# Attention scores: the low-key matmuls of two heads in the two halves of the TensorE array

## The chip, the cores and the metric

The kernel runs on one core of a Trainium2 chip. TensorE (PE) multiplies, VectorE (DVE), ScalarE (ACT) and GpSimd (POOL) do the elementwise work, SyncE (SP) and the others issue the DMAs. The metric is the device time of one launch in microseconds (us); before the change its median over 3 runs was 724.25 us (724.15 to 724.58).

## What is computed

One decoder block over 512 positions of 1024 channels, in float32. The part that the change touches is the attention with three kinds of keys (8 heads of 64 channels, two groups of 4 heads that share keys):

```python
def masked_softmax(s, mask):
    p = jax.nn.softmax(jnp.where(mask, s, NEG), axis=-1)
    return jnp.where(mask, p, 0.0)

# for a block of 128 query positions:
sc = einsum('bqghd,bkgd->bghqk', qc, k_cmp) * scale       # compressed keys
p_c = masked_softmax(sc, cmp_end <= t);  o_c = einsum(p_c, v_cmp)
...
ss = einsum('bqghd,bgqkd->bghqk', qc, ks) * scale         # selected blocks of keys
p_s = masked_softmax(ss, kpos <= t);     o_s = einsum(p_s, vs)
...
sw = einsum('bqghd,bkgd->bghqk', qc, kw) * scale          # sliding window of keys
p_w = masked_softmax(sw, mask_w);        o_w = einsum(p_w, vw)
out = gc[..., 0:1] * o_c + gc[..., 1:2] * o_s + gc[..., 2:3] * o_w
```

With 512 positions there are 8 blocks of 64 keys and up to 16 may be selected, and the window is 512 wide, so both branches see all keys up to the query; they differ in their keys and values. Around this stand a gated short convolution, a merge of the two mixers, and a feed-forward layer with a convolution (2816 channels).

## The kernel before

Precision comes from splitting: a float32 value becomes a high part (a rounded copy) and a low part (the rest), and a product is the sum of high x high, low x high and high x low. The helper `dense` does so with three matmuls per unit (lines 140, 143, and 145 or 147).

For scores, the 64 channels of a head fill only half of the array's 128 rows, and the query operand uses both halves: tile `q` (in the trace `qT`) holds for each head the high part of the query in one half of the partitions, `own`, and the low part in the other. Group 0 has its high part in the lower half, group 1 in the upper half. The keys lie in `kk`: `kHH` has the high part of the keys in both halves, and `kL` has the low part in the half where the query's high part lies and zeros in the other, written by two memsets (line 584). So two matmuls give a head's scores (`scores`, lines 714 and 715): q against `kHH` makes high x high + low x high in one pass, and q against `kL` makes high x low.

The operands are made in `qkv`, token tile by token tile (128 positions, `tt` 0 to 3): transposes into PSUM (`pqt`, line 681), then for each group a copy of the high part (ACT, 686), a subtraction for the low part of the query (DVE, 689), two copies of the keys' high part (ACT, 692 and 693), and a subtraction for the keys' low part (DVE, 694). The compressed keys are made once in `compress` (lines 623 to 625).

`attend(pt_, g, qt)` handles one group and one query tile; tiles go in the order 3, 2, 1, 0. Tile 3 has 512 keys, tile 2 384, and in tiles 2 and 1 the branch 0 takes the 32 compressed keys with it (416 and 288 columns); tile 3 makes its compressed scores apart (`pcm`, line 725), and tile 0 does both branches in one matmul (line 753). Each head's scores take one of three PSUM banks `s` (`s_bank`). `exps` adds the causal mask (DVE, 741), takes the maximum (DVE, 742) and the exponential (ACT, 743), which frees the bank. Then the weights are scaled (769), transposed (`pt`, 792), split (`ph` 795, `pl` 796) and multiplied by the values (800 to 805). The compressed weights take a way of their own (`xs` 782, `ptc` 785).

The framework's scheduler sets the order of instructions on each engine ahead of time, from program order and simulated times; `behind(later, earlier)` adds an order without a semaphore, and `tc.high_priority()` raises an instruction's place. During attention PE also does the convolution's products (`pa`), the merge gates (`pg`) and the mixer's output (`pma`), which need nothing of attention. Of the last gate before the merge (`gate_tile(KD + 4)`) three units are ordered behind the last transposes and value products of attention (`HOLD_PTC`, `HOLD_PT`, `HOLD_PO`).

Of the kernel before, what the change touches and what calls it, by code (L numbers as in the profile page):

```python
# [11 lines left out]
F32 = mybir.dt.float32  # L12
F32R = mybir.dt.float32r
I32 = mybir.dt.int32
AF = mybir.ActivationFunctionType
# [9 lines left out]
G = 2  # L25
HG = H // G
HD = 64
# [7 lines left out]
NC = S // STRIDE  # L35
# [56 lines left out]
def tile_block(ctx: ExitStack, tc: tile.TileContext, xT, pos, par, par2, w_tok, w_a3, w_gate, w_ao, w_bo, w_o,  # L92
               w_ff, w_dn, c_w1, out):
    nc = tc.nc
# [28 lines left out]
    def s_bank(name):  # L123
        return bank("s", name, 3)
# [8 lines left out]
    loads, splits = [], []  # L133
# [186 lines left out]
    def behind(later, earlier):  # L320

        tc.add_manual_dep(later.ins, earlier.ins.name,
                          mybir.DependencyInfo(mybir.DependencyClass.NoSync, mybir.DependencyReason.DATA),
                          reason="order")
# [204 lines left out]
    kHH, kL = kk[:, 0], kk[:, 1]  # L529
    kl4 = kL.rearrange("p (b g) s -> p b g s", g=G)  # L530
# [22 lines left out]
    def compress():  # L553

        ph = s_bank("ph")
        hb = w_tmp("hb", (7, 2 * NC))
        z, e, hid = (hb[:, i] for i in range(3))
        peb = pp.tile([P, 1], F32, name="peb", tag="peb")

        half = 2 * G * (NC + 1)  # L560
        hl = ph[:, 0:2 * half].rearrange("p (s n) -> p s n", s=2)
        blocks = kc2s.rearrange("p b s a k g -> p b s (a k g)")
        for i in range(2):
            wh, wl = load_w(c_w1[:, :, 8 * i:8 * i + 8], D, f"w1{i}", mixed=True)
            for n in range(8):
                x = blocks[:, n, :, 2 * G * i:2 * G * i + half]
                c = slice(n * P, (n + 1) * P)
                nc.tensor.matmul(hl, wh[:, c], x, start=i + n == 0, stop=False)
                nc.tensor.matmul(hl[:, 0], wl[:, c], x[:, 0], start=False, stop=i == 1 and n == 7)
        h = hl[:, 0].rearrange("p (n a g) -> p a g n", a=2, g=G)  # L570
        tmp = hb[:, 3:6].rearrange("p a n -> p (a n)")[:, 0:half]
        nc.scalar.activation(tmp, hl[:, 1], AF.Copy)
        nc.vector.tensor_add(hl[:, 0], hl[:, 0], tmp)
        for kv in range(2):
            rows = slice(kv * HD, (kv + 1) * HD)
            nc.vector.tensor_copy(peb[rows], h[rows, kv, 0, NC:])
            nc.vector.tensor_scalar(z[rows].rearrange("p (g n) -> p g n", g=G), h[rows, kv, :, 0:NC], peb[rows], None,
                                    op0=ALU.add)
        nc.scalar.activation(e, z, AF.Tanh, scale=0.5)
        nc.vector.tensor_scalar(e, e, 0.5, 0.5, op0=ALU.mult, op1=ALU.add)  # L580
        nc.vector.tensor_mul(hid, z, e)
        for g in range(G):
            rows = slice((1 - g) * HD, (2 - g) * HD)
            (nc.vector if g else nc.gpsimd).memset(kl4[rows, :, g].bitcast(F32), 0.0)

        nc.gpsimd.memset(kk[:, :, G:, 0:NC].bitcast(F32), 0.0)
        for b in range(2):
            rows = slice((1 - b) * HD, (2 - b) * HD)
            nc.vector.memset(vc_t[rows, b].bitcast(F32), 0.0)
        pc = ph[:, 0:2 * P]  # L590

        nc.tensor.matmul(pc[:, 0:HD], hb[:, 1:3].rearrange("p a n -> p (a n)"), w2k, start=True, stop=True)

        hd4 = hb[:, 3:7].rearrange("p a n -> p (a n)").rearrange("p (g a n) -> p g a n", g=G, a=4)
        hv = hid.rearrange("p (g n) -> p g n", g=G)
        nc.vector.tensor_copy(hd4, hv[:, :, None, :].to_broadcast([P, G, 4, NC]))
        src = lambda g: pc[:, (1 + g) * HD:(2 + g) * HD]
        for g in range(G):
            nc.tensor.matmul(src(g), hd4[:, g].rearrange("p a n -> p (a n)"), w2v, start=True, stop=True)
        kc = pp.tile([2 * NC, HD], F32, name="kcmp", tag="kcmp")  # L600
        nc.vector.tensor_copy(kc, pc[2 * NC:, 0:HD])
        for g in range(G):
            for b in range(2):
                rows = slice(b * HD, (b + 1) * HD)
                v = vc_t[rows, b, g, :]
                nc.scalar.activation(v[:, 0:HD], src(g)[rows], AF.Copy)
                nc.vector.tensor_sub(v[:, HD:], src(g)[rows], v[:, 0:HD].bitcast(F32))
        s_ = pp.tile([2 * NC, HD], F32, name="kcmp2", tag="kcmp2")
        ss = pp.tile([2 * NC, 2], F32, name="kss", tag="kss")
        nc.gpsimd.tensor_mul(s_, kc, kc)  # L610
        nc.vector.reduce_sum(ss[:, 0:1], s_, axis=AX.X)
        nc.vector.tensor_scalar(ss[:, 0:1], ss[:, 0:1], 1.0 / HD, EPS, op0=ALU.mult, op1=ALU.add)
        nc.gpsimd.tensor_tensor(ss[:, 1:2], ss[:, 0:1], mhalf[0:2 * NC, 0:1], op=ALU.pow)
        nc.vector.scalar_tensor_tensor(kc, kc, ss[:, 1:2], g_sb[0:2 * NC, 1, :], op0=ALU.mult, op1=ALU.mult)
        st = pp.tile([P, 2 * HD], F32R, name="kst", tag="kst")
        nc.vector.memset(st[2 * NC:].bitcast(F32), 0.0)
        nc.vector.tensor_copy(st[0:2 * NC, 0:HD], kc)
        nc.vector.tensor_sub(st[0:2 * NC, HD:], kc, st[0:2 * NC, 0:HD].bitcast(F32))
        pt = ph[:, 2 * P:3 * P]
        nc.tensor.transpose(pt, st.bitcast(F32), ident)  # L620
        for g in range(G):
            gs = slice(g * NC, (g + 1) * NC)
            nc.scalar.activation(kHH[0:HD, g, 0:NC], pt[0:HD, gs], AF.Copy)
            nc.scalar.activation(kHH[HD:, g, 0:NC], pt[0:HD, gs], AF.Copy)
            nc.vector.tensor_copy(kL[g * HD:(g + 1) * HD, g, 0:NC], pt[HD:, gs])


    v_t = const([P, NT, 4, P], "v_t", F32R, pb)
# [12 lines left out]
    def qkv(tt, a, tp):  # L641
# [28 lines left out]
        q = pb.tile([P, H, P], F32R, name=f"qT{tt}", tag="qT", bufs=NT)  # L670
        qT[tt] = q
        ks = slice(NC + tt * P, NC + (tt + 1) * P)
        kh = kHH.rearrange("p (b g) s -> p b g s", g=G)
        halves = [slice(g * HD, (g + 1) * HD) for g in range(G)]
        for b in range(2):

            n = 4 - 2 * b
            pv = tp(f"pqt{tt}{b}").rearrange("p (h t) -> p h t", t=P)[:, 0:n]
            for i in range(n):
                src = t1[:, 8 * b + 2 * i:8 * b + 2 * i + 2].rearrange("p h d -> p (h d)")  # L680
                nc.tensor.transpose(pv[:, i, :], src, ident)
            for g in range(G):
                own, other = halves[g], halves[1 - g]
                if b == 0:
                    qg = q[:, 4 * g:4 * g + 4]
                    m = nc.scalar.activation(qg[own], pv[own], AF.Copy)
                    if tt < 2:
                        behind(m, splits[-1])
                    nc.vector.tensor_sub(qg[other], pv[own], qg[own].bitcast(F32))
                else:  # L690
                    kg = kh[:, :, g, ks]
                    nc.scalar.activation(kg[own], pv[own], AF.Copy)
                    nc.scalar.activation(kg[other], pv[own], AF.Copy)
                    nc.vector.tensor_sub(kl4[own, :, g, ks], pv[own], kg[own].bitcast(F32))


    yb_h = y_tile("yb_h").rearrange("p a c -> p (a c)")[:, 0:4 * S].rearrange("p (a s) -> p a s", a=4)
# [4 lines left out]
    def attend(pt_, g, qt):  # L702
        nk = (qt + 1) * P
        off = NC if qt < NT - 1 else 0
        q = qT[qt]
        gates = gate_n[:, qt, g * HG * 3:(g + 1) * HG * 3].rearrange("p (h b) -> p h b", b=3)
        tag = f"{g}{qt}"
# [1 line left out]
        def small(name, n, dt=F32):  # L709
            return pt_.tile([P, HG, n], dt, name=f"{name}{tag}", tag=name, bufs=2)  # L710

        def scores(w, i, br, a, b):
            h = g * HG + i
            nc.tensor.matmul(w, q[:, h, :], kHH[:, 2 * br + g, a:b], start=True, stop=False)
            nc.tensor.matmul(w, q[:, h, :], kL[:, 2 * br + g, a:b], start=False, stop=True)

        def scale_of(sums, br):
            nc.vector.reciprocal(sums, sums)
# [17 lines left out]
        def exps(i, br, sc, o):  # L736
            e, mx, sums = parts[br]
            if o:
                nc.vector.tensor_add(xc[:, i, :], sc[:, 0:NC], cm_add[:, qt, :])
            dg = sc[:, o + nk - P:o + nk]  # L740
            nc.vector.tensor_add(dg, dg, causal)
            nc.vector.tensor_reduce(mx[:, i], sc[:, o:o + nk], axis=AX.X, op=ALU.max, negate=True)  # L742
            nc.scalar.activation(e[:, i, 0:nk], sc[:, o:o + nk], AF.Exp, bias=mx[:, i], accum_out=sums[:, i])  # L743

        both = 2 * (NC + nk) <= S
        if both:
# [3 lines left out]
            for i in range(HG):  # L750
                sc = s_bank(f"sc{tag}{i}")[:, 0:2 * (NC + nk)].rearrange("p (b n) -> p b n", b=2)
                for j, k in enumerate((kHH, kL)):
                    nc.tensor.matmul(sc, q[:, g * HG + i, :], k.rearrange("p (b g) s -> p b g s", g=G)[:, :, g, 0:NC + nk],
                                     start=j == 0, stop=j == 1)
                for br in (1, 0):
                    exps(i, br, sc[:, br] if br == 0 else sc[:, br, NC:], NC if br == 0 else 0)
        for br in (1, 0):
            o = off if br == 0 else 0
            if not both:
                part(br)  # L760
                for i in range(HG):
                    sc = s_bank(f"sc{tag}{i}{br}")
                    scores(sc[:, 0:o + nk], i, br, NC - o, NC + nk)
                    exps(i, br, sc, o)
            e, mx, sums = parts[br]
            scale_of(sums, 1 + br)
            for i in range(HG):
# [2 lines left out]
            if br == 0:  # L770
# [12 lines left out]
                pt = t_bank(f"ptc{tag}")  # L783
# [508 lines left out]
```

## Time and profile before

| | |
|---|---|
| median of 3 runs | 724.25 us |
| the profiled execution | 725.49 us, of it 723.6 us from the first to the last instruction |
| busy: PE, DVE, ACT, POOL | 716.9, 575.6, 415.3, 125.4 us |
| granted TensorE clock | 1.000 |
| making of query and key tiles | about 57 to 98 us |
| attention | about 99 to 293 us |
| feed-forward layer | about 378 us to the end |

A line of the trace names the engine, the line of the kernel, the operation, the tile written and those read, and shapes as partitions x elements. For matmuls, `128*128` are rows and columns of the array in use and `128x512` the output. PEld is the load of the stationary operand, which runs beside matmuls. Matmuls overlap in the pipe: one of 512 columns is listed with about 0.39 us, but the next begins earlier, so the distance between starts is what one costs. Lists of waits give total us, times, and the longest.

### The profile page before, as it was taken

The page shows a single profiled execution, that of the slowest core. Times are in us where ns is not written, and L with a number is a line of the kernel's source. Part 1 is how long each engine was busy: PE and PEld are TensorE (multiplying, and loading weights), DVE is VectorE, ACT ScalarE, POOL GpSimd, SP SyncE. Part 2 cuts the span into 40 slices and gives each one's busy share as a digit, 9 for nine tenths or more (in the row PEclk, how much of TensorE's full clock was granted, in tenths as well). Part 3 has the DMA queues.
Part 4 walks back from the last instruction along what each step waited for, and adds up shares of the span by engine and source line. Part 5 has one row for each costly group of instructions (what it writes and reads, how often), then busy time and mean ns, then how long its engine had stood idle before and what let it go on. Part 6 is the DMA issues. An engine that isn't in the chain of part 4 may idle for free.

```text
span 723.6 us, 11196 instructions
## 1 busy us (share of the span) xinstructions
PE 716.9 (99%) x4275; PEld 637.1 (88%) x4275; DVE 575.6 (80%) x988; ACT 415.3 (57%) x706; POOL 125.4 (17%) x111
## 2 busy tenths in 40 slices
PE   8999999999999999999999999999999999999997
PEld 8999788888888888878889999999999999999986
DVE  7978967587666675887876998998898988989833
ACT  7776555777767767544665665565445554455320
POOL 1122443343343201231002011010000010000000
PEclk9999999999999999999999999999999999999999
DMA  8633552211111211336446476545655556552413
GB/s 292 227 89 115 145 119 79 60 68 58 59 59 59 87 60 59 116 124 210 160 131 161 117 175 152 169 119 131 164 143 127 136 127 154 128 146 88 117 30 116
DMA packets 36804, 88.19 MB, mean 122 GB/s; under 512 B 7440, under 2 KB 10896, under 8 KB 36752
## 3 DMA queue, kind: packets, MB, share of 16 engines
q1 hardware_dynamic: 30672, 74.42, 32.3%
q0 software_dynamic: 5648, 12.58, 10.7%
q8 instruction: 33, 0.54, 0.3%
q10 hardware_dynamic: 432, 0.49, 0.2%
q14 instruction: 19, 0.16, 0.1%
HBM read 85.39 MB, written 2.10 MB: 121 GB/s over the span
## 4 chain that ended last, share of the span: by engine, by line
PE 92%; issue 4%; DMA 2%; POOL 0%; ACT 0%; DVE 0%; SPq 0%; POOLq 0%; DVEq 0%
PE p L147 8%; PE p L143 8%; PE p L140 8%; PE pdn L143 4%; PE pdn L140 4%; PE pg L145 4%; PE pg L140 4%; PE pg L143 4%; PE pdn L147 4%; PE pa L140 3%; PE pa L143 3%; PE pt L792 2%; PE po L143 2%; PE po L140 2%; PE po L147 2%
## 5 line engine op out<-in xcount | busy, mean ns | idle before, releaser
L140 PE MATMUL p<-xf_h,sh 128*128 128x256 f32 x352 | 87.3, 281 | 0.0
L143 PE MATMUL p<-xf_l,sh 128*128 128x256 f32 x352 | 87.2, 281 | 0.0
L140 PEld LDWEIGHTS p<-xf_h,sh 128*128 128x128 f32 x352 | 66.3, 188 | 0.0
L143 PEld LDWEIGHTS p<-xf_l,sh 128*128 128x128 f32 x352 | 66.3, 188 | 0.0
L930 DVE TENSOR_TENSOR sl<-s,sh 128x1024 fp32r<-128x1024 f32 x44 | 53.1, 1214 | 3.9 <-ACT sh L929 3.9
L147 PE MATMUL p<-xf_h,sl 128*128 128x256 f32 x352 | 55.8, 281 | 0.0
L929 ACT ACTIVATE sh<-s 128x1024 fp32r<-128x1024 f32 x44 | 45.6, 1051 | 17.4 <-DVE s L974 13.2
L955 POOL DMA_DIRECT2D wl_d<-in_w_dn_dram x16 | 19.1, 1195 | 207.2 <-ACT wl_d L952 207.2
L143 PE MATMUL pdn<-al,wh_d 128*128 128x512 f32 x134 | 52.6, 393 | 0.0
L140 PE MATMUL pdn<-ah,wh_d 128*128 128x512 f32 x134 | 52.2, 392 | 0.0
L140 PE MATMUL pg<-xg_h,wh_g 128*128 128x512 f32 x128 | 51.0, 399 | 0.0
L145 PE MATMUL pg<-xg_h,wl_g 128*128 128x512 f32 x128 | 50.8, 397 | 0.0
L143 PE MATMUL pg<-xg_l,wh_g 128*128 128x512 f32 x128 | 50.5, 395 | 0.0
L147 PEld LDWEIGHTS p<-xf_h,sl 128*128 128x128 f32 x352 | 47.9, 188 | 0.3
L743 ACT ACTIVATE e<-sc,mx 128x512 f32<-128x512 f32 (+3 forms) x64 | 33.3, 525 | 18.8 <-DVE mx L742 16.4
L140 PE MATMUL p<-xf_h,wh_s 128*128 128x256 f32 x176 | 43.5, 280 | 0.0
L143 PE MATMUL p<-xf_l,wh_s 128*128 128x256 f32 x176 | 43.4, 281 | 0.0
L140 PE MATMUL pa<-xg_h,wh_a 128*128 128x512 f32 x96 | 38.2, 398 | 0.0
L143 PE MATMUL pa<-xg_l,wh_a 128*128 128x512 f32 x96 | 37.9, 395 | 0.0
L796 DVE TENSOR_TENSOR pl<-pt,ph 128x512 fp32r<-128x512 f32 x40 | 27.3, 685 | 10.8 <-ACT ph L795 10.4
L769 ACT ACTIVATE e<-e,sums 128x512 f32<-128x512 f32 (+3 forms) x64 | 30.9, 556 | 7.5 <-DVE sums L719 7.5
L929 ACT ACTIVATE th<-wr_s 128x512 fp32r<-128x512 f32 x20 | 12.6, 630 | 38.7 <-issue 28.3
(361 smaller groups left out, 2133.5 us busy)
## 6 DMA issues: line engine op xcount, KB each, us to landing
wr_s<-in_w_ff_dram SPq DMA_DIRECT2D x44, 512.0 KB, 3.6
wr_d<-in_w_dn_dram SPq DMA_DIRECT2D x22, 512.0 KB, 3.7
wr_g<-in_w_gate_dram SPq DMA_DIRECT2D x16, 512.0 KB, 3.5
wl_d<-in_w_dn_dram POOLq DMA_DIRECT2D x16, 512.0 KB, 7.0
wr_a<-in_w_a_dram SPq DMA_DIRECT2D x12, 512.0 KB, 3.5
wr_t<-in_w_tok_dram SPq DMA_DIRECT2D x10, 524.0 KB, 5.8
wr_o<-in_w_o_dram SPq DMA_DIRECT2D x8, 512.0 KB, 3.7
wr_ao<-in_w_ao_dram SPq DMA_DIRECT2D x4, 512.0 KB, 3.5
```

The lines of the kernel that those rows point to most:

```text
L140: m = nc.tensor.matmul(acc, wh, xh, start=first and i == 0, stop=False)
L143: nc.tensor.matmul(acc, wh, xl, start=False, stop=False)
L145: m = nc.tensor.matmul(acc, wl, xh, start=False, stop=last and i == n - 1)
L147: m = nc.tensor.matmul(acc, wl, xh, start=False, stop=last and i == n - 1)
L743: nc.scalar.activation(e[:, i, 0:nk], sc[:, o:o + nk], AF.Exp, bias=mx[:, i], accum_out=sums[:, i])
L769: nc.scalar.activation(v, v, AF.Copy, scale=sums[:, i])
L792: ends["pt"] = nc.tensor.transpose(pt[:, i * P:(i + 1) * P], e[:, i, kt * P:(kt + 1) * P], ident)
L796: m = nc.vector.tensor_sub(pl, pt, ph.bitcast(F32))
L929: m = nc.scalar.activation(h, v, AF.Copy)
L930: nc.vector.tensor_sub(l, v, h.bitcast(F32))
L955: nc.gpsimd.dma_start(view(l), src, accum_op=ALU.add)
```

## The change

For query tiles 3 and 2 the scores of two heads are made together, in two `s` banks: first the two high matmuls (full height), then the two low matmuls, each over only the 64 rows in which its head has its high part. For the two to lie in different halves, every second head has its halves exchanged: heads 0 and 2 of a group keep the high part in `own`, heads 1 and 3 have it in `other`. The low matmul of the second head goes first, that of the first head behind it; `behind` keeps the order and `high_priority` lifts the low ones. Tiles 1 and 0 and the compressed scores of tile 3 keep their matmuls over all rows.

`kL` now has the low keys in both halves: an ACT copy to the other half for each key tile and group, two casts per group instead of one for the compressed keys, and no memsets. Where a matmul over all rows meets `kL`, it now adds low x low as well. The query's copies and subtractions are issued for two heads each instead of four.

```diff
@@ compress
-        for g in range(G):
-            rows = slice((1 - g) * HD, (2 - g) * HD)
-            (nc.vector if g else nc.gpsimd).memset(kl4[rows, :, g].bitcast(F32), 0.0)
...
-            nc.vector.tensor_copy(kL[g * HD:(g + 1) * HD, g, 0:NC], pt[HD:, gs])
+            nc.vector.tensor_copy(kL[0:HD, g, 0:NC], pt[HD:, gs])
+            nc.vector.tensor_copy(kL[HD:, g, 0:NC], pt[HD:, gs])
@@ qkv
-                    m = nc.scalar.activation(qg[own], pv[own], AF.Copy)
-                    if tt < 2:
-                        behind(m, splits[-1])
-                    nc.vector.tensor_sub(qg[other], pv[own], qg[own].bitcast(F32))
+
+                    for i, (hi, lo) in enumerate(((own, other), (other, own))):
+                        hs = slice(i, 4, 2)
+                        m = nc.scalar.activation(qg[hi, hs], pv[own, hs], AF.Copy)
+                        if tt < 2:
+                            behind(m, splits[-1])
+                        nc.vector.tensor_sub(qg[lo, hs], pv[own, hs], qg[hi, hs].bitcast(F32))
...
                     nc.vector.tensor_sub(kl4[own, :, g, ks], pv[own], kg[own].bitcast(F32))
+                    nc.scalar.activation(kl4[other, :, g, ks], kl4[own, :, g, ks].bitcast(F32), AF.Copy)
@@ attend
-        def scores(w, i, br, a, b):
+        def scores(ws, i, br, a, b):
             h = g * HG + i
-            nc.tensor.matmul(w, q[:, h, :], kHH[:, 2 * br + g, a:b], start=True, stop=False)
-            nc.tensor.matmul(w, q[:, h, :], kL[:, 2 * br + g, a:b], start=False, stop=True)
+            if len(ws) == 1:
+                nc.tensor.matmul(ws[0], q[:, h, :], kHH[:, 2 * br + g, a:b], start=True, stop=False)
+                nc.tensor.matmul(ws[0], q[:, h, :], kL[:, 2 * br + g, a:b], start=False, stop=True)
+                return
+
+            for n, w in enumerate(ws):
+                high = nc.tensor.matmul(w, q[:, h + n, :], kHH[:, 2 * br + g, a:b], start=True, stop=False)
+            for n in reversed(range(len(ws))):
+                rows = slice((g + n) % 2 * HD, ((g + n) % 2 + 1) * HD)
+                with tc.high_priority():
+                    m = nc.tensor.matmul(ws[n], q[rows, h + n, :], kL[rows, 2 * br + g, a:b], start=False, stop=True)
+                behind(m, high)
+                high = m
...
-                for i in range(HG):
-                    sc = s_bank(f"sc{tag}{i}{br}")
-                    scores(sc[:, 0:o + nk], i, br, NC - o, NC + nk)
-                    exps(i, br, sc, o)
+                n = 2 if qt > 1 else 1
+                for i in range(0, HG, n):
+                    sc = [(s_bank if m < 3 else t_bank)(f"sc{tag}{i + m}{br}") for m in range(n)]
+                    scores([b[:, 0:o + nk] for b in sc], i, br, NC - o, NC + nk)
+                    for m in range(n):
+                        exps(i + m, br, sc[m], o)
```

## The prediction

> **What bounds the kernel now.** I read the page's head first, then the chain that ended last, PE's own waits, and the windows around the two stages that the change touches.
>
> ```profile
> span 723.6 us, 11196 instructions
> ...
> PE 716.9 (99%) x4275; PEld 637.1 (88%) x4275; DVE 575.6 (80%) x988; ACT 415.3 (57%) x706; POOL 125.4 (17%) x111
> ...
> PE 92%; issue 4%; DMA 2%; POOL 0%; ACT 0%; DVE 0%; SPq 0%; POOLq 0%; DVEq 0%
> ```
> ```profile
> PE wu L195 <- POOL ones L191: 1.1, 1, 1.1
> PE p L147 <- DMA wl_s<-in_w_ff_dram: 1.0, 1, 1.0
> PE pj_s L240 <- DVE xg_h L292: 0.8, 1, 0.8
> ```
> ```profile
> 57.00:100.00 43.00, 43.00 (x231) 37.09 (x230) 36.34 (x77) 26.91 (x51) 14.19 (x12) 1.00 0.52 132
> 97.00:290.00 193.00, 193.00 (x965) 160.63 (x965) 132.79 (x339) 132.69 (x317) 59.32 (x46) 1.00 0.21 66
> ```
>
> The reader is to see one thing: TensorE is the program. Its 717 us fill the span, the chain is PE for 92%, and its listed waits come to 2.9 us, none of them on a score. In the attention window (97 to 290 us) PE is busy for 193.00 of 193 us while DVE and ACT work 132.8 and 132.7 us of it; in the window where the query and key tiles are made (57 to 100 us) PE again has no gap, DVE is at 36.3 and ACT at 26.9 of 43. So an edit there counts as PE time, and DVE and ACT work counts only if it makes PE wait. Busy PE is a modelled figure, so I price matmuls by the distance of their starts, not by their durations.
>
> **What the change takes off PE.** The scores are these groups:
>
> ```profile
> L714 PE MATMUL sc<-kk,qT x48: 279/380/481, 99.8 to 246.4; 128*128 128x512 f32 x16, 128*128 128x384 f32 x8, 128*128 128x416 f32 x8, 128*128 128x256 f32 x8
> L715 PE MATMUL sc<-kk,qT x48: 274/351/477, 100.3 to 246.5; 128*128 128x512 f32 x16, 128*128 128x384 f32 x8, 128*128 128x416 f32 x8, 128*128 128x256 f32 x8
> ```
> ```profile
> 110.37 0.40 PE L715 MATMUL sc<-kk,qT 128*128 128x512 f32 x1
> 110.60 0.39 PE L714 MATMUL sc<-kk,qT 128*128 128x512 f32 x1
> 110.83 0.39 PE L715 MATMUL sc<-kk,qT 128*128 128x512 f32 x1
> 111.06 0.39 PE L143 MATMUL pa<-xg_l,wh_a 128*128 128x512 f32 x1
> ```
> ```profile
> 180.53 0.33 PE L714 MATMUL sc<-kk,qT 128*128 128x384 f32 x1
> 180.70 0.34 PE L715 MATMUL sc<-kk,qT 128*128 128x384 f32 x1
> 180.88 0.39 PE L140 MATMUL pg<-xg_h,wh_g 128*128 128x512 f32 x1
> ...
> 191.34 0.35 PE L715 MATMUL sc<-kk,qT 128*128 128x416 f32 x1
> 191.53 0.35 PE L714 MATMUL sc<-kk,qT 128*128 128x416 f32 x1
> 191.72 0.35 PE L715 MATMUL sc<-kk,qT 128*128 128x416 f32 x1
> 191.91 0.40 PE L143 MATMUL pg<-xg_l,wh_g 128*128 128x512 f32 x1
> ```
>
> L714 multiplies the whole query operand (high and low half) by the high keys; L715 multiplies it by the low-key operand kL, half of whose rows are zero. From start to start one takes 0.231 us at 512 columns (110.37 to 111.06 in three steps is 0.69, so 0.230), 0.175 at 384 (180.53 to 180.88 in two) and 0.19 at 416 (191.34 to 191.91 in three). The last two query tiles, qt 3 and 2, hold the 16 of 512 columns (qt 3, both branches), the 8 of 384 and the 8 of 416 (qt 2). After the change these 32 run as 16 pairs, each pair in opposite halves of the array: 8 pairs of 512, 4 of 384, 4 of 416. The columns streamed otherwise stay the same: L714 is untouched, and tiles 1 and 0 keep their full matmuls, now with a low-times-low product in rows that were zero, at the same columns.
>
> If the two of a pair run wholly beside each other, one whole matmul per pair goes: 8 x 0.231 + 4 x 0.175 + 4 x 0.19 = 3.31 us. That is the end of the gain. By the Trainium skill, "TensorE: Matmul & The Clock Gate", section Part 3: Packing small matmuls — row/col tiling, matmuls in different row groups start about 4 ns apart, which would give 16 x 0.004 less, 3.25 us; no row of this trace shows two matmuls side by side.
>
> I don't take that whole. The second of the pair needs weights of its own, and what a load costs that no long matmul covers shows where narrow matmuls follow each other, each with a load:
>
> ```profile
> 263.92 0.40 PE L805 MATMUL po<-pl,v_t 128*128 128x512 f32 x1
> 264.15 1.03 PE L792 MATMUL pt<-ident,e 128*128 128x128 f32 x8
> ```
> ```profile
> L792 PE MATMUL pt<-ident,e x160: 270/272/274, 120.8 to 289.5; 128*128 128x128 f32 x160
> ...
> 110.37 0.19 PEld L714 LDWEIGHTS sc<-kk,qT 128*128 128x128 f32 x1
> ```
>
> Eight transposes of 128 columns with eight loads last 1.03 us, the last one alone 0.272 (the shape's median), so (1.03 - 0.27) / 7 = 0.108 us each. In the present order each load starts when the matmul ahead of its own starts: the load at 110.37 is for the L714 of 110.60, and 110.37 is the start of the L715 before it. The first load of a pair so lies under the high matmul before it. If the second starts only with the first low matmul, that pair's second half starts 0.108 us after the first: the pair lasts 0.108 longer than one matmul. Saved: 8 x (0.231 - 0.108) + 4 x (0.175 - 0.108) + 4 x (0.19 - 0.108) = 0.98 + 0.27 + 0.33 = 1.58 us. Between 0 and 3.31 us this is my term, as the load is the one thing that each of the two still needs for itself.
>
> Going from full-height to half-height matmuls and back happens twice per pair, 32 times. The trace has no such change. The lower bound is 0, and the nearest row is the change between transposes and matmuls, another kind of use of the array: from 263.92 (L805) to the matmul behind the eight transposes nothing sticks out of 0.23 + 8 x 0.11. The upper bound is that the array has to run empty: a 512-column matmul is listed with 0.393 us and gives way after 0.231, so 0.162 us per change, 32 x 0.162 = 5.2 us. I take 0, by the nearer row; the other end is the rival of the other sign.
>
> **What it adds elsewhere.** Rows of the stage that makes the operands:
>
> ```profile
> L686 ACT ACTIVATE qT<-pqt x8: 574/594/596, 57.7 to 95.4; 64x512 fp32r<-64x512 f32 x8
> L692 ACT ACTIVATE kk<-pqt x8: 361/367/374, 58.2 to 96.0; 64x256 fp32r<-64x256 f32 x8
> L689 DVE TENSOR_TENSOR qT<-pqt,qT x8: 683/689/694, 59.2 to 96.3; 64x512 fp32r<-64x512 f32 x8
> L694 DVE TENSOR_TENSOR kk<-pqt,kk x8: 405/419/428, 59.9 to 97.4; 64x256 fp32r<-64x256 f32 x8
> ```
> ```profile
> L625 DVE CAST kk<-ph x2: 194/195/196, 105.2 to 107.1; 64x32 fp32r<-64x32 f32 x2
> L584 DVE MEMSET kk<- x1: 965/965/965, 1.2 to 1.2; 64x1088 f32 x1
> L584 POOL MEMSET kk<- x1: 999/999/999, 2.3 to 2.3; 64x1088 f32 x1
> ```
>
> Each copy and subtraction of four heads becomes two of two heads. ACT: 2 x 0.367 for 0.594, +0.14, eight times: 1.1 us. DVE: 2 x 0.419 for 0.689, +0.15, eight times: 1.2 us. The copy of the low keys into the other half is eight new ACT instructions of 64x256, at the 0.367 of that shape 2.9 us. Two more casts on DVE, 0.4 us. Together ACT +4.0, DVE +1.6 us over 57 to 107 us, some 1.3 us for one token tile. I cost this at nothing: PE streams projections and convolution products (pa) meanwhile, and both engines have room. Without that cover the last tile's 1.3 us would delay the first scores. The new ACT copy waits on the DVE subtraction ahead of it; queued behind it on ACT are the next group's copies and the weight split wh_a, whose reader on PE then is late by at most the 0.42 of that subtraction; I take 0, as PE's list shows no wait on wh_a. The two memsets leave at 1 to 3 us; PE's one wait there is on ones, which POOL writes before its memset, so they give nothing; if they gave all, 1 us.
>
> The scores of two heads now hold two of the three score banks. The third head's high matmul finds the third bank, the fourth needs the first head's bank back, and the low ones of both stand behind it. So the third head's maximum and exponential start later by one head's work at most:
>
> ```profile
> L742 DVE TENSOR_REDUCE mx<-sc x64: 276/474/692, 103.9 to 282.1; 128x1 f32<-128x512 f32 x16, 128x1 f32<-128x384 f32 x16, 128x1 f32<-128x256 f32 x16, 128x1 f32<-128x128 f32 x16
> L743 ACT ACTIVATE e<-sc,mx x64: 344/524/694, 105.3 to 283.4; 128x512 f32<-128x512 f32 x16, 128x384 f32<-128x384 f32 x16, 128x256 f32<-128x256 f32 x16, 128x128 f32<-128x128 f32 x16
> ```
>
> That is 0.69 + 0.69 = 1.4 us, eight times (second pair of 2 tiles x 2 groups x 2 branches). If PE stood still for it, 11 us; but behind PE's score matmuls the program has pa, pg and pma products that need nothing of attention, and today no score appears among PE's waits. I take 0. No DMA is moved, and no queue of SP or POOL is passed.
>
> **The sum.** The profiled execution took 725.49 us (723.6 of span and 1.9 around it), 1.2 above the median of 724.25. 725.49 - 1.58 = 723.9 for such an execution, and 724.25 - 1.58 = 722.7 us for the median.
>
> **The rivals.**
>
> *Full overlap*: both loads lie under the high matmul (0.231 us holds two of 0.108). Gain 3.31 us: 720.9. For it, the room; against it, that loads in this trace start one matmul ahead.
>
> *Slower: the change of height empties the array.* With 0.162 per change and the pairs as in my sum: 724.25 - 1.58 + 5.18 = 727.9; with full overlap 724.25 - 3.31 + 5.18 = 726.1, which I take as its time, since an empty array leaves both loads open to run early. It decides from 0.05 us per change (1.58 / 32), and is slower by over 0.2% from 0.095. For it: a matmul's listed length beyond its pitch; against it: the transposes, which come and go at no price. The Trainium skill's "TensorEngine Tiling (Array Packing)", section Tiling Modes, speaks for it: changing the tiling mode, not just the tile, drains TensorE. No run here shows that yet, and the page gives no time for it.
>
> *No gain*: the halves run one behind the other, or the gain is lost at the tail. For the second, the last attention tile:
>
> ```profile
> 278.99 0.30 DVE L741 TENSOR_TENSOR sc<-sc,causal 128x128 f32<-128x128 f32 x1 [2.12 <-PE sc L753]
> ...
> 285.89 0.29 DVE L782 TENSOR_TENSOR xs<-xc,xs 128x128 fp32r<-128x128 f32 x1 [0.92 <-ACT xs L781]
> ```
> ```profile
> 287.20 0.25 PEld L785 LDWEIGHTS ptc<-ident,xs 128*128 128x128 f32 x2
> ```
>
> xs is ready at 286.18 and its transpose's load starts at 287.20, 1.0 us later. If DVE and ACT didn't come earlier at all, PE could gain only this 1.0 us: 723.2. If the halves run in turn, 724.3. Against the tail: DVE itself waited 2.12 us for a score there, so an earlier PE also draws the vector engines forward.
>
> **How the numbers follow.** A measurement of this kernel tells about 0.2%, 1.45 us, from no change. Staggered pairs (forecast, 722.7, own range 721.9 to 723.6): 0.32. Full overlap: 0.24. No gain (723.2 to 724.6): 0.20. Slower through the change of height (725.7 to 727.9): 0.24. Faster by over 0.2% is below 722.8: all of full overlap and 0.19 of the forecast's 0.32, so 0.43. Same: 0.13 + 0.20 = 0.33. Slower: 0.24. The range goes from near full overlap, 720.9, to 726.1, and leaves out about 0.15.
>
> **What would show it.** In the changed trace the low score matmuls of tiles 3 and 2 appear with 64 rows. The forecast holds if the second starts some 0.11 us after the first and the next full matmul about 0.34 us after the first (at 512 columns); full overlap if it's 0.23; the slower rival if the first of a pair starts later than 0.231 after the high matmul, or the next full one 0.16 beyond the pair's end. PE's waits should gain no line on sc, qT or ptc; a line of over 1 us there makes the prediction wrong in its covers. A start of attention later than 99.8 us by 1 us or more would show the copies uncovered.

## The result, and the profile after

The changed kernel takes 733.58 us (733.09 to 734.57, 4 runs) against 724.41 us before (724.15 to 724.64, 4 runs): a ratio of 1.0128, 95% interval 1.0111 to 1.0146. It is 9.2 us slower. The forecast was 722.7, the range ended at 726.1, so the result lies outside, on the side of the rival "the change of height empties the array", and 7.5 us beyond the time that I gave it.

The page of the changed kernel, its head:

```profile
span 730.9 us, 11220 instructions
...
PE 722.2 (99%) x4275; PEld 635.1 (87%) x4275; DVE 575.7 (79%) x997; ACT 418.9 (57%) x722; POOL 125.2 (17%) x110
```

PE has as many instructions as before and is busy 5.3 us longer; DVE's total is unchanged and ACT has 3.6 us more. PE's own waits, before three lines of about 1 us, have three new lines, two from the end of attention and one from the making of its operands; the wait of 1.0 us for the DMA of `wl_s` is gone:

```profile
PE po L815 <- DVE yo L827: 2.3, 1, 2.3
...
PE pa L140 <- ACT wh_a L171: 0.6, 1, 0.6
PE po L815 <- ACT ph L810: 0.5, 1, 0.5
```

Three places can be read from this trace.

The first is the pairs. The low matmuls are there with 64 rows, and the two of a pair stand in one row of the timeline, as two. PE, then the weight loads (PEld), of the changed kernel:

```profile
100.17 0.40 PE L722 MATMUL sc<-kk,qT 128*128 128x512 f32 x1
100.49 0.50 PE L726 MATMUL sc<-kk,qT 64*128 64x512 f32 x2
100.92 0.50 PE L143 MATMUL pa<-xg_l,wh_a 128*128 128x512 f32 x1
101.26 0.40 PE L140 MATMUL pa<-xg_h,wh_a 128*128 128x512 f32 x1
101.49 0.40 PE L143 MATMUL pa<-xg_l,wh_a 128*128 128x512 f32 x1
```
```profile
111.00 0.18 PEld L726 LDWEIGHTS sc<-kk,qT 64*128 64x128 f32 x2 [0.37 <-issue]
111.43 0.19 PEld L722 LDWEIGHTS sc<-kk,qT 128*128 128x128 f32 x1 [0.25 <-issue]
111.54 0.19 PEld L145 LDWEIGHTS pa<-xg_h,wl_a 128*128 128x128 f32 x1
```

The two of a pair start 3 to 4 ns apart, at 512, 416 and 384 columns alike (read from the instructions' own starts): they do run side by side. But the pair starts 0.32 us after the high matmul instead of 0.23, the next full-height matmul 0.43 after the pair, and the one behind it 0.34 after that. Together 1.09 us, where the four whole matmuls that stood there took 0.92: a 512-column pair costs 0.17 us more than it replaces. The loads say where: those of the pair start at 111.00, when the pair itself starts (its row in the timeline of PE is also 111.00), after 0.37 us with no load, and the first full-height load behind it at 111.43, again with its matmul. Before, the load came one matmul ahead. The next load begins only 0.11 later, at 111.54, and its matmul 0.23 behind it, at 111.77: so the second start behind a change of height is late as well, by about 0.1 us, and of the price of a change about half falls on each of the two. The same lateness of the second start follows a wait of PE (69.27 to 69.60 is 0.33 us), so it goes with a load that wasn't ahead, not with half height alone.

The second is the end of attention (PE, changed kernel):

```profile
288.54 1.89 PE L807 MATMUL pt<-ident,e 128*128 128x128 f32 x8
290.94 0.50 PE L815 MATMUL po<-ph,v_t 128*128 128x512 f32 x1 [0.50 <-ACT ph L810]
291.27 0.40 PE L819 MATMUL po<-pc,vc_t 128*128 128x256 f32 x2
291.66 0.49 PE L820 MATMUL po<-pl,v_t 128*128 128x512 f32 x1
294.44 0.77 PE L815 MATMUL po<-ph,v_t 128*128 128x512 f32 x1 [2.28 <-DVE yo L827]
295.00 0.63 PE L820 MATMUL po<-pl,v_t 128*128 128x512 f32 x1
295.43 0.63 PE L800 MATMUL ptc<-ident,xs 128*128 128x128 f32 x2
295.85 1.06 PE L807 MATMUL pt<-ident,e 128*128 128x128 f32 x4
296.56 0.78 PE L140 MATMUL pg<-xg_h,wh_g 128*128 128x512 f32 x1
```

From 288.5 to 296.5 no gate product (pg) stands between attention's last steps. Before, they stood between the transposes of the last tile:

```profile
286.88 0.60 PE L792 MATMUL pt<-ident,e 128*128 128x128 f32 x4
...
287.45 0.48 PE L140 MATMUL pg<-xg_h,wh_g 128*128 128x512 f32 x1
...
289.16 0.60 PE L792 MATMUL pt<-ident,e 128*128 128x128 f32 x4
289.52 0.48 PE L140 MATMUL pg<-xg_h,wh_g 128*128 128x512 f32 x1
```

In the changed kernel PE waits 0.5 and 2.3 us for the chain through ACT and DVE, and what comes behind runs slowly: the two value products start 0.56 and the next 0.43 us apart, the gate product at 296.56 is 0.58 us ahead of the following one. The columns after the five busy times in these windows are granted clock, DMA share and GB/s:

```profile
286.00:292.00 6.00, 5.40 (x26) 3.66 (x24) 3.19 (x14) 4.23 (x16) 0.12 (x1) 1.00 0.00 0
292.00:298.00 6.00, 3.72 (x14) 3.04 (x14) 2.32 (x7) 3.77 (x9) 1.47 (x3) 0.72 0.02 4
```

The clock granted to TensorE has a mean of 0.72 in the six microseconds from 292, which hold the gap itself. In shorter windows it is 1.00 up to 294, while PE stands still, and then half for about 3.4 us:

```profile
295.00:296.00 1.00, 1.00 (x5) 0.79 (x4) 0.00 (x0) 0.00 (x0) 0.56 (x1) 0.50 0.07 16
297.00:298.00 1.00, 1.00 (x5) 0.75 (x5) 0.54 (x1) 0.91 (x2) 0.00 (x0) 0.75 0.00 0
```

Before, that place had PE busy for 6.00 of 6 us at 1.00:

```profile
290.00:296.00 6.00, 6.00 (x28) 4.93 (x28) 3.56 (x5) 2.36 (x4) 1.28 (x1) 1.00 0.32 89
```

If one adds up what the distances of starts on PE are above the median of their shape, 275 to 300 us holds 6.3 us of excess, and 0.5 before: 5.8 us lost there.

The third is small: at 69 us PE waits 0.6 us for a weight split (`wh_a` in the list of waits).

### The profile page after: what moved, and what is told of

The parts are those of the page before. It is cut to its first block, busy times and chain, and to the rows that moved or that the text cites. A ratio compares the mean times of both kernels' runs of the same rounds, so it can differ in the third digit from the quotient of the medians.

```text
span 730.9 us, 11220 instructions
## 1 busy us (share of the span) xinstructions
PE 722.2 (99%) x4275; PEld 635.1 (87%) x4275; DVE 575.7 (79%) x997; ACT 418.9 (57%) x722; POOL 125.2 (17%) x110
## 4 chain that ended last, share of the span: by engine, by line
PE 96%; ACT 2%; DVE 1%; DMA 0%; issue 0%; SPq 0%; DVEq 0%
PE p L143 10%; PE p L147 10%; PE p L140 10%; PE pdn L143 4%; PE pdn L140 4%; PE pg L140 4%; PE pg L145 4%; PE pg L143 4%; PE pdn L147 4%; PE pa L140 3%; PE pa L143 3%; PE pt L807 2%; PE po L140 2%; PE po L143 2%; PE po L147 2%; PE pa L145 2%
## 5 line engine op out<-in xcount | busy, mean ns | idle before, releaser
L147 PE MATMUL pdn<-ah,wl_d 128*128 128x512 f32 x128 | 34.7, 393 | 0.0
```

The costliest lines, as they stand in the source:

```text
L147: m = nc.tensor.matmul(acc, wl, xh, start=False, stop=last and i == n - 1)
```

## The experiments

Theory A: two large causes, the change of height at the pairs and an order at the end of attention that leaves PE without work. Theory B: the change of height alone, the gap being what follows from later scores. Theory C: the operand copies. All medians below stand beside runs of the kernel before on the same chip.

**All pairs, full height.** One edit; the order of instructions on all five engines stays that of the changed kernel.

```diff
-                rows = slice((g + n) % 2 * HD, ((g + n) % 2 + 1) * HD)
+                rows = slice(0, P)
```

> The changed kernel with one edit: the low matmuls of a pair go over all 128 rows. Every engine has the same instructions in the same order as in the changed kernel. In the changed kernel's trace a 512-column pair costs 0.326 + 0.003 + 0.425 + 0.337 = 1.09 us from the high matmul ahead of it to the second start behind it, where four whole matmuls take 0.924, so 0.17 us too much; with the narrower pairs some 3 us in all. Theory A (two causes: the change of height, and an order at the end of attention that leaves PE with nothing to do): only the 3 us go, 730.6 us, and PE's gap of over 2 us near 292 us stays. Theory B (the change of height alone, the gap being its consequence): back to 724 to 725 us, no gap.

Measured: 730.82 us against 723.81, ratio 1.0096 (1.0081 to 1.0111). The gap of 2.3 us on `yo` stayed to the digit. So without any half-height matmul 7.0 of the 9.2 us are still there, and B falls. The price of the 16 pairs is best read inside the two traces, whose PE order is the same. Rows of the score tile, the changed kernel, then this one:

```profile
L722 PE MATMUL sc<-kk,qT x32: 337/398/500, 99.0 to 215.2; 128*128 128x512 f32 x16, 128*128 128x384 f32 x8, 128*128 128x416 f32 x8
...
L717 PE MATMUL sc<-kk,qT x16: 279/292/387, 216.0 to 253.9; 128*128 128x256 f32 x8, 128*128 128x288 f32 x8
```
```profile
L722 PE MATMUL sc<-kk,qT x32: 335/393/481, 99.0 to 212.4; 128*128 128x512 f32 x16, 128*128 128x384 f32 x8, 128*128 128x416 f32 x8
...
L717 PE MATMUL sc<-kk,qT x16: 279/290/379, 213.0 to 250.8; 128*128 128x256 f32 x8, 128*128 128x288 f32 x8
```

Both make the first score at 99.0; tile 1's first score (L717) comes at 216.0 with half height and at 213.0 without. The pairs cost 3.0 us net of the matmuls that they save.

**Half height with no partner.** In the kernel before, for tiles 3 and 2:

```diff
-            nc.tensor.matmul(w, q[:, h, :], kL[:, 2 * br + g, a:b], start=False, stop=True)
+            nc.tensor.matmul(w, (q[g * HD:(g + 1) * HD] if qt > 1 else q)[:, h, :], (kL[g * HD:(g + 1) * HD] if qt > 1 else kL)[:, 2 * br + g, a:b], start=False, stop=True)
```

> The kernel before with one edit: the 32 low matmuls of tiles 3 and 2 go over the 64 rows that aren't zero, one at a time, with no partner. Same instructions in the same order on every engine as before. Theory A: each costs one change of height there and one back, 1.09 - 3 x 0.231 = 0.40 us, 32 x 0.40 = 12.8 us: 737 us, and no long gap at the end of attention. Theory B the same price, but with a gap of microseconds at the end of attention on top: 741 us or more. If a change of height were free: 724.4 us.

Measured: 736.50 against 723.81, ratio 1.0172 (1.0155 to 1.0189): 12.7 us, 0.40 for each of 32. PE waits nowhere over 1.1 us: here scores 12 us later open no gap at the end of attention. Four rows show the price where high and low matmuls follow each other:

```profile
110.94 0.48 PE L714 MATMUL sc<-kk,qT 128*128 128x512 f32 x1
111.35 0.49 PE L715 MATMUL sc<-kk,qT 64*128 64x512 f32 x1
111.78 0.50 PE L714 MATMUL sc<-kk,qT 128*128 128x512 f32 x1
112.21 0.49 PE L715 MATMUL sc<-kk,qT 64*128 64x512 f32 x1
```

One every 0.43 us instead of 0.23: 0.2 us for each change of height, in either direction. In the pairs above it is the same 0.2, spread over two starts: 0.10 at the pair, 0.20 behind it (the rest of the first change and the start of the second), 0.10 at the next.

**Pairs for tile 3 only.**

```diff
-                n = 2 if qt > 1 else 1
+                n = 2 if qt > 2 else 1
```

> The changed kernel with pairs for query tile 3 alone (8 pairs of 512 columns); here the last tile's transposes stand between gate products again, as before. Theory A: 8 x 0.17 = 1.3 us, 725.8 us, no gap. Theory B (loss in proportion to the pairs): about half of the 9.2 us, 729 us.

Measured: 727.70 against 723.81, ratio 1.0054 (1.0039 to 1.0069): 3.9 us, between the two figures. A's number missed the operand copies (next run, 2.0 us), and its "no gap" missed a shorter gap that is here too, in spite of the better order:

```profile
PE po L815 <- DVE yo L827: 1.4, 1, 1.4
```

**Operands only.** The same line as `n = 1`.

> The changed kernel with no pairs: exchanged halves, low keys in both halves, no memsets, but every head's scores by two matmuls over all rows as before. Theory A: 724.4 us within 0.7. Rival C (the added copies on ACT and DVE make attention late): 727 us or more, with PE waits on sc or qT.

Measured: 725.77 against 723.81, ratio 1.0028 (1.0018 to 1.0037): 2.0 us, between the two figures: A was 0.7 beyond its margin, and C's loss is smaller and without its waits on sc or qT. The new waits are others:

```profile
PE po L815 <- ACT ph L810: 0.7, 1, 0.7
PE pa L140 <- ACT wh_a L171: 0.6, 1, 0.6
```

The excess over the shapes' medians is 0.8 us more than before at 50 to 75 us and 1.0 more at 275 to 300. Pairing at full height (730.82) adds 5.1 us to this kernel; the excess at 275 to 300 us is 6.5 there and 1.5 here, which is those 5.0.

Why pairing costs this at the end of attention, even with every matmul over all rows, shows in the gate products. 312 of them stand ahead of the merge. The rows give those of tile `pg` from the start to the last score: the kernel before, operands only, pairs for tile 3 only, and all pairs at full height. The first x is the number on PE:

```profile
0.00:278.60 278.60, 67.48 (x265) 48.77 (x265) 6.88 (x10) 1.00 0.34 104
0.00:279.20 279.20, 69.12 (x268) 48.86 (x268) 6.86 (x10) 1.00 0.32 104
0.00:283.20 283.20, 71.98 (x276) 50.69 (x277) 6.83 (x10) 1.00 0.32 103
0.00:283.30 283.30, 72.47 (x288) 53.20 (x288) 6.84 (x10) 1.00 0.32 104
```

That leaves 47, 44, 36 and 24 for the rest of attention, and the excess at 275 to 300 us grows as they fall: 0.5, 1.5, 2.2 and 6.5 us. The 20 that pairing used up earlier are 4.6 us of PE at 0.231. They went into tiles 3 and 2: from the first score to tile 1's first takes 106.0 us with the operands only (99.3 to 205.3) and 114.0 with pairs at full height (99.0 to 213.0).

**More fill at the end of attention.** Gate 5 is made beside gates 2 to 4 and takes over the ties that gate 4 had.

```diff
-GATES_AT = ((2, 3, 4), (5,), (6,), (7,))
+GATES_AT = ((2, 3, 4, 5), (), (6,), (7,))
...
-            args = (s_bank, {HOLD_PTC: ends["ptc"], HOLD_PT: ends["pt"], HOLD_PO: ends["po"]}) if j == 4 else ()
+            args = (s_bank, {}) if j == 4 else (s_bank, {HOLD_PTC: ends["ptc"], HOLD_PT: ends["pt"], HOLD_PO: ends["po"]}) if j == 5 else ()
```

> The changed kernel with more work for PE at the end of attention: gate 5 is made beside gates 2 to 4, and the orders that tie a gate's units behind the last transposes and value products go from gate 4 to gate 5, so gate 4's 24 matmuls are free to stand between them. Same work in all. Theory A (gap from the order there): no gap near 290 us, PE matmuls there at 0.23 us; before plus about 0.8 us (operand copies at 50 to 75 us) plus 2.2 to 3.0 us (16 pairs), 726.8 to 727.8 us. Rival (the last tiles' chain through DVE and ACT is late whatever PE has to do): a gap of 2 us or more stays and the time is 731 us or more.

Measured: 730.75 against 723.92, ratio 1.0091 (1.0076 to 1.0107). The gap near 290 us is gone: PE is busy throughout at full clock, with gate products between the last transposes:

```profile
275.00:300.00 25.00, 25.00 (x123) 20.42 (x122) 15.99 (x55) 17.44 (x53) 3.44 (x6) 1.00 0.16 56
```

Here 48 gate products are left at the last score instead of 24. The time missed A's figure by 3 us. Of that 2.1 are a new wait: the merge products of a later pair stand still for DVE, probably because the moved gate is missing where it came from.

```profile
310.10 0.50 PE L140 MATMUL pmb<-yb_h,wh_bo 128*128 128x512 f32 x1 [2.06 <-DVE tb L1044]
310.43 0.39 PE L143 MATMUL pmb<-yb_l,wh_bo 128*128 128x512 f32 x1
310.66 0.39 PE L145 MATMUL pmb<-yb_h,wl_bo 128*128 128x512 f32 x1
```

The four executions differ in the granted clock: 729.4 and 729.9 us at 1.000 (the profiled one is the latter), 731.6 and 731.8 at 0.998.

**The same fill, full height.** The run above with `rows = slice(0, P)`; again the same order on every engine.

> The run with more fill, and its low matmuls over all 128 rows; every engine in the same order as there. The difference of the two is the price of the 16 pairs with nothing else changed: theory A 2.2 to 3.0 us less, 724.5 to 725.3 us. If half height gained anything, this one would be slower than its partner.

Measured: 726.87 against 723.92, ratio 1.0037 (1.0023 to 1.0051), 3.9 us less than its partner, more than the 2.2 to 3.0 expected; against the partner's two executions at clock 1.000 it is 2.8. Inside the traces the stretch from the first score to tile 1's first takes 116.9 us with half height (99.5 to 216.4) and 114.0 without (99.3 to 213.3): 2.9 us, as above. Its own 2.9 us over the kernel before are about the 0.8 us of the copies and the 2.0 us of the wait on tb, which it shares.

**The copy of the low keys by GpSimd,** in the operands-only kernel:

```diff
-                    nc.scalar.activation(kl4[other, :, g, ks], kl4[own, :, g, ks].bitcast(F32), AF.Copy)
+                    nc.gpsimd.tensor_copy(kl4[other, :, g, ks], kl4[own, :, g, ks].bitcast(F32))
```

> The operands-only kernel with the copy of the low keys to the other half on GpSimd instead of ACT. If the 2.0 us of that kernel come from ACT's longer queue (PE waited 0.6 us for a split wh_a behind those copies), about 1 us goes: 724.6 us, no PE wait on wh_a. If the order at the end of attention makes them: 725.8 us or any other, with the loss at 280 to 295 us.

Measured: 724.86 against 723.92, ratio 1.0010 (1.0000 to 1.0019). About 1 us went, but the wait on wh_a only fell to 0.4, and the excess at 275 to 300 us went with the new order. What share each had can't be told from this run.

**Four heads at a time,** with the added fill: `n = 4 if qt > 1 else 1`.

> The run with more fill, and four heads at a time instead of two: four high matmuls, then four low ones in two pairs, one change of height there and one back for four heads. A look at starts: theory A says the second pair starts about 0.23 us after the first, no dearer than whole matmuls, and the changes cost 0.1 us before and about 0.3 us behind as with two heads; 8 groups then cost 4 x (0.40 - 0.46) + 4 x (0.40 - 0.37) = -0.1 us against whole matmuls. Attention will be slower with all score banks taken, and PE will miss work at its end, so the whole is slower than 728 us.

Measured once: 763.7 us. The end is as starved as foreseen (granted clock 0.83 from 250 to 300 us), the gate products stop at 268 us, before tile 1's first score at 278.6, and none of the 48 left starts before 320. Tile 1's scores wait 5.3 us in all for exponentials, which free the banks. What it was run for, the four low matmuls in a row:

```profile
137.02 0.40 PE L722 MATMUL sc<-kk,qT 128*128 128x512 f32 x1
137.35 0.73 PE L726 MATMUL sc<-kk,qT 64*128 64x512 f32 x4
138.01 0.50 PE L820 MATMUL po<-pl,v_t 128*128 128x512 f32 x1
138.35 0.38 PE L800 MATMUL ptc<-ident,xs 128*128 128x128 f32 x2
```

The four last 0.73 us, one matmul alone 0.39, so the second pair starts 0.34 us after the first, not 0.23: A's figure for it was too low. But the next start comes 0.32 after the second pair, where behind a single pair it takes 0.43. The second pair is the second start behind the change, which was late by 0.1 in the rows above too, so its lateness is that of the change; a pair behind a pair pays nothing of its own here. From the high matmul to the second start behind the pairs it is 1.33 us, and six whole matmuls take 6 x 0.231 = 1.39. So one way there and back costs 0.40 for two pairs as for one, and two pairs of 512 columns come out 0.06 us ahead, as A's sum had it. This is one group in one trace: the other groups of this kernel have waits or narrower matmuls around them.

**Gate 4 not tied.** The changed kernel with `(s_bank, {})` for gate 4.

> The changed kernel without the orders that tie gate 4's units behind the last transposes and value products. In its order 18 of gate 4's 24 matmuls stand ahead of the products that PE waited 2.3 us for, and none stands behind the last transposes. Theory A (ready work was kept behind the tie): the 2.3 us wait goes, but the last transposes, their copies and subtractions then run with PE idle for 1 to 2 us: 730 to 732 us against 733.6. Rival (attention's end is late by itself and the tie plays no part): 733 us or more, with the same wait in the same place.

Measured: 733.30 against 724.06, ratio 1.0126 (1.0101 to 1.0150): no gain. The 2.3 us wait went, and others took its place, with slow matmuls behind them:

```profile
296.19 0.66 PE L807 MATMUL pt<-ident,e 128*128 128x128 f32 x4 [0.49 <-DVE pl L811]
...
298.95 0.50 PE L815 MATMUL po<-ph,v_t 128*128 128x512 f32 x1 [1.11 <-ACT ph L810]
300.49 0.80 PE L143 MATMUL pmb<-yb_l,wh_bo 128*128 128x512 f32 x1 [0.57 <-POOL yb_l L830]
```

The time is the rival's, but the wait didn't stay in its place: the loss only moved. So the tie isn't the cause. As in the changed kernel 24 gate products are left at the last score, too little for the end of attention, with the tie or without; the run with a whole gate more is the one that closed that gap.

No run beat the kernel before. A single pair of 512 columns, the widest there is, already loses; two in a row about break even, but the groups of four heads that they need cost far more at the end of attention.

## Why the prediction was wrong, step by step

**"I take 0" for the change of height** was the first step that failed. It was put between 0 and 0.162 us a change, and 0 was taken from transposes that come and go freely. They use the whole array; they say nothing of a change of rows. The reading of those rows also stopped one start early: the second start behind the eight transposes comes 0.32 us after the first, 0.09 over the pitch.

```profile
264.94 0.48 PE L143 MATMUL pg<-xg_l,wh_g 128*128 128x512 f32 x1
265.26 0.39 PE L145 MATMUL pg<-xg_h,wl_g 128*128 128x512 f32 x1
```

Measured: 0.2 us per change (12.7 us for 64 changes in the single half-height run), above my upper end. That end counted the run-out of the pipe only, and not the weight load, which comes out of hiding as well, in both directions, as the PEld rows show. How the 0.2 divides between run-out and load can't be told, as the ends of matmuls are modelled.

The rule that I weighed against it, from the Trainium skill's "TensorEngine Tiling (Array Packing)", section Tiling Modes, that a change of tiling mode drains TensorE, agrees with these runs as far as they go: they show the late starts and late loads, 0.2 us per change, but not the draining itself.

**The pair itself** was better than the forecast's staggered start: 3 to 4 ns apart, so a whole matmul was saved, the 3.31 us of full overlap. The Trainium skill's "TensorE: Matmul & The Clock Gate", section Part 3: Packing small matmuls — row/col tiling, gives about 4 ns, and the trace agrees. Gain 3.3 us, price 16 x 0.4 = 6.4, net 3.1; inside the traces 3.0 was measured. The rival had the right place, and its 1.87 us was too small.

**"If PE stood still for it, 11 us ... I take 0"**, the two banks held at once, is the step with the larger loss. The reason given, that pa, pg and pma products stand behind the scores, held for the scores themselves: no score is among PE's waits. It overlooked that these products are a fixed amount, used up by about 293 us even before. The 11 us were not far off as a delay: with pairs at full height tiles 3 and 2 take 8.0 us longer than with the operands alone. PE didn't stand still for it, but it paid in gate products, which were then missing at the end: 24 left instead of 44. Pairing at full height cost 5.1 us over the operands alone, all of it at 275 to 300 us. That paired scores hold two of three banks is the likely reason for the delay; the orders that the edit adds (`behind`, `high_priority`) are another, and no run separated the two, as none gave the pairs another score bank.

**The tail rival** (723.2 us at worst) saw the place and mis-sized it: it only asked what an earlier PE could lose of the gain, never that the order there is made anew by the scheduler. The order before had gate products between the last transposes; the order after has none for 8 us. And it counted no clock: from the end of the gap the granted clock was half for 3.4 us.

**"I take 0, as PE's list shows no wait on wh_a"**: the list was that of the kernel before, whose ACT queue was shorter. The split was late by 0.6 us where I had bounded it at 0.42. Operands alone cost 2.0 us against 0.

**Right** were the price of a whole matmul by distance of starts, the memsets (nothing at 1 to 3 us), and that SP's queue and the DMAs would add no wait. As differences of medians the shares are 2.0 for the operands, 5.1 for the pairing and 2.2 for the height; they give the 9.2 because each is the difference to the run before. Read inside the traces, on its own, the height is 3.0. The profiled executions differ by less, 7.3 us of span (730.9 against 723.6), partly because the 1.0 us wait for `wl_s` is missing in the changed kernel's.

## What to carry to other kernels

Two half-height matmuls side by side are worth one whole matmul, but going to half height and back costs 0.4 us here, more than a 512-column matmul's 0.23. One pair at a time loses 0.17 us; two in a row saved 0.06 in the one group that shows it, and longer rows weren't run. Where a scheduler fills one engine with independent work, that fill is a budget: count what is left of it where the chain that it covers ends, and price any edit that lengthens that chain by the gap that opens there. An order that is planned anew is a change of its own; comparing kernels with the same order on all engines, as three pairs of kernels here could, separates the edit from it.

## What the runs showed that I had not expected

Waits of 0.5 and 2.3 us on PE were followed by a granted clock of half for 3.4 us, and 512-column matmuls behind them started 0.4 to 0.6 us apart instead of 0.23; with this, the 2.8 us of waits went with 5.8 us of loss. But a gap doesn't always do so: after 2.06 us in the profiled execution of the run with more fill, and after 3.1 us in the run with four heads (340.7 to 343.9), matmuls started 0.23 apart again from the second on, at clock 1.00. What decides it, these runs don't show.

And a weight load lay under the matmul ahead while both had the same height; at a change of height it began with its own matmul, and this one and the next were each about 0.1 us late. Between two half-height pairs it stayed hidden: with four heads all four loads were over at 137.65 us, and the second pair started at 137.69.
